# Class-C values move to the first two slots of a causal mixer, gates take their place, and a minimum is pinned

## The chip, the cores and the metric

The kernel runs on one core of a Trainium2 chip. The metric is the device time of one execution in microseconds. A core has five engines with queues of their own, each in order: TensorE for matrix products (PE; PEld are its weight loads), VectorE (DVE), ScalarE (ACT), GpSimd (POOL) and SyncE (SP), whose queue issues most DMAs. Products go to PSUM, which has eight banks of 128 x 512 floats.

## The reference

One decoder layer on 512 tokens of width 1024, in fp32. After an RMSNorm, one projection W_in feeds three mixers and three gates per channel:

- A: twelve heads of causal, dilated attention in three groups (dilation 1, 4, 16). Head slot j of all three groups is combined by the softmax denominators.
- B: a gated linear recurrence of width 512.
- C: eight heads of causal attention over blocks of 256.

```
gt = sigmoid(gates)
merged = gt[0]*(o_a @ p_a) + gt[1]*(o_b @ p_b) + gt[2]*(o_c @ p_c)
x = x + merged @ w_out
x = x + (silu(gate) * up) @ w_down        # gate, up from rms_norm(x) @ w_gu
```

A last RMSNorm follows. A and C add a relative-position bias from one table.

## The kernel before, in words

Every fp32 product is made of three: both operands are split into a rounded high part and the low rest (hi, lo), and `mm3` adds hi·hi, hi·lo and lo·hi. A weight chunk of 128 x 1024 is loaded by SP (`wraw`), rounded on ScalarE (`whi`, L177) and its rest taken on GpSimd, or on VectorE for the first and last chunks (`wlo`, L178). `chunk_plan` lists the chunks in the order of their use; three buffers hold raw chunks and four the split ones, so the loader runs two chunks ahead.

The projections of mixer A start before the norm is known: they run on `X`, the raw input times the norm's weights, and the norm's factor is applied when a result leaves PSUM. `norm_tok` makes the factor per token (`r_tok`), `norm_all` spreads it by two matmuls over all partitions (`rb`, L359, L361). Later `renorm` multiplies a second copy of the input, which `reload` fetches, by `rb` (L924) and splits it (L244, L245) into `XN`; all later projections run on `XN`. `bias_rows` multiplies the bias table with one-hot rows (L391), adds a mask (L393) and writes the rows to DRAM; `bias_tile` reads shifted tiles back through SP's queue (L401).

Mixer A goes by four head slots, d0 to d3. For one slot j:

- `ea` (through `fa`) evicts a projection of queries or keys into tiles (L469 to L524).
- `la` makes the logits of the three groups: group 0 by L554, L555 and the reduction L562, groups 1 and 2 by L576, L579 and the reductions L585. `stn` and `stp` take the minima (the logits are negated).
- `wa` takes exponentials (L594) and sends minima and sums to DRAM (`exch`, issued on ScalarE at L717), from where SP's queue reads them back in the other group's token order (L719).
- `wa2` takes the minimum over both (`mm`, L725), its factors (df, ee, wd, ds, rd, ff; L727 to L740), and scales the tiles P by them (L599).
- `ta` transposes P on TensorE (L608, L622) and `xa` multiplies with the values (L659, L777).

`weave(gen, n, steps, first)` runs a projection of n steps and puts the given steps between its matmuls, evenly, after the first `first`. `class_values_g` makes the values of groups 1 and 2, `values_g` four token blocks of one value projection in 32 steps of three matmuls, on `X` for group 0 and on `XN` for mixer C (`VC`, used later by `tc_`). A gate is a projection of 24 matmuls with a tanh behind it; `early(place)` makes as many gates as the table EARLY lists, and what is left of the 24 is made in the merge.

The engines' orders are not those of the program text: a scheduler moves instructions within each engine's queue where no dependence forbids it, by its own estimate of times. `tc.keep_in_program_order` holds one instruction at its place in the text. PSUM banks are taken as they come free: a product that needs one waits for the engine that empties it. TensorE's queue is in order, so everything behind such a product waits too.

Of the kernel before, what the change touches and what calls it, by code (L numbers as in the profile page):

```python
# [43 lines left out]
N_POOL = 62  # L44
AHEAD = 2

EARLY = {"a2": 1, "a3": 1, "v0": 1, "v1": 1, "c0": 1, "c1": 1, "l1": 1, "l2": 1, "l3": 1, "l4": 1,
         "b0": 1, "b1": 4}
G_LEAD = 2
N_WARM = 10  # L50
# [5 lines left out]
def chunk_plan():  # L56

    plan = []

    def a(h, i, w):  # L60
        plan.append(("ma", (OFF_QA, OFF_KA)[w], A_PAIRS[h][i]))

    def v(off, g):
        plan.extend(("v", off + g * 256, kh) for kh in range(2))

    def c(m, w):
        plan.append(("m", "w_in", (OFF_QC, OFF_KC)[w] + m * 128))

    def b(m):
        plan.append(("m", "w_in", OFF_XB + m * 128))  # L70
        plan.append(("m", "w_in", OFF_GB + m * 128))

    gates = [("m", "w_in", OFF_GT + n * D + m * 128) for m in range(8) for n in range(3)]

    def g(place):
        for _ in range(EARLY[place]):
            plan.append(gates.pop(0))

    for n in (0, 1):
        a(0, n, 0)  # L80
        a(0, n, 1)
    v(OFF_VA, 0)
    plan.extend(("vv", OFF_VA + 256, kq) for kq in range(4))
    a(0, 2, 0)
    a(0, 2, 1)
    for n in range(2):
        a(1, n, 0)
        a(1, n, 1)
    a(1, 2, 0)
    g("a2")  # L90
    a(1, 2, 1)
    g("a3")
    v(OFF_VC, 0)
    g("v0")
    v(OFF_VC, 1)
    c(0, 0)
    g("v1")
    c(0, 1)
    g("c0")
    c(1, 0)  # L100
    c(1, 1)
    g("c1")
    for m in (2, 3):
        c(m, 0)
        g("l1" if m == 2 else "l3")
        c(m, 1)
        g("l2" if m == 2 else "l4")
    b(0)
    g("b0")
    plan.append(("lru",))  # L110
    for m in range(1, 4):
        b(m)
    g("b1")
    np_ = 0
    for m in range(8):
        while gates and 24 - len(gates) < 3 * m + 3 + G_LEAD:
            plan.append(gates.pop(0))
        while np_ * 8 < (m + 1) * 10:
            plan.append(("p", np_))
            np_ += 1  # L120
    for m in range(8):
        plan.append(("m", "w_out", m * 128))
    for m in range(FT):
        plan.append(("m", "w_gu", m * 128))
        plan.append(("m", "w_gu", FFN + m * 128))
    for k in range(FT):
        plan.append(("d", k))
    return plan


def layer_kernel(tc, x0p, xT, wts, tab, oneh, msk, idn, gfin, out):
# [4 lines left out]
    with (  # L136
# [20 lines left out]
        def f32(ap):  # L157
            return ap.bitcast(F32)
# [40 lines left out]
        def weave(gen, n, steps=(), first=0):  # L199

            done = 0
            i = 0
            while True:
                try:
                    next(gen)
                except StopIteration as e:
                    for st in steps[done:]:
                        st()
                    return e.value
                i += 1  # L210
                while done < len(steps) and i - first >= (done + 1) * (n - first) / (len(steps) + 1):
                    steps[done]()
                    done += 1
# [205 lines left out]
                        yield  # L419
            return [[ps[:, g * 256 : g * 256 + 256] for ps in pss] for g in range(2)]  # L420

        def values_g(act=X):
            ch = [chunk("v"), chunk("v")]
            outs = []
            for tb in range(4):
                if tb % 2 == 0:
                    ps = bank()
                o = ps[:, (tb % 2) * 256 : (tb % 2) * 256 + 256]
                outs.append(o)
                t = slice(tb * 128, (tb + 1) * 128)  # L430
                for k in range(8):
                    hi, lo = ch[k // 4]
                    c = slice((k % 4) * 256, (k % 4) * 256 + 256)
                    xh, xl = act[k]
                    mm3(o, xh[:, t], xl[:, t], hi[:, c], lo[:, c], k == 0, k == 7)
                    yield
            return outs

        def values_mm(steps=(), first=0, act=X):
            return weave(values_g(act), 32, steps, first)  # L440

        def values_out(outs, perm=False, scaled=False):
            res = []
            for tb, o in enumerate(outs):
                o4 = o.rearrange("p (h e) -> p h e", h=4)
                v = slot(F32R, "v")
                v4 = v.rearrange("p (h two e) -> p h two e", two=2, e=E)
                if scaled:
                    nc.scalar.copy(v4[:, :, 0, :], o4)
                    nc.vector.tensor_sub(v4[:, :, 1, :], o4, f32(v4[:, :, 0, :]))  # L450
                    res.append(v)
                    continue
                rt = r_tok[:, tb + 4 * perm : tb + 4 * perm + 1]
                nc.scalar.activation(v4[:, :, 0, :], o4, AF.Copy, scale=rt)
                nc.vector.scalar_tensor_tensor(
                    v4[:, :, 1, :], in0=o4, scalar=rt, in1=f32(v4[:, :, 0, :]),
                    op0=ALU.mult, op1=ALU.subtract,
                )
                res.append(v)
            return res  # L460
# [200 lines left out]


        VA = []
        qk = {}
        exch = dr.tile([4, 4 * 512], F32)

        def ea(ps, half, i, w, scaled=False):
            pair = A_PAIRS[half][i]
            perm = [g > 0 for g, _ in pair]
            r = None if scaled else (rq, rb)[w]  # L670
            t = (q_tiles, k_tiles)[w](ps, r, perm)
            for n in range(2):
                qk[pair[n] + (w,)] = t[n]

        def fa(half, i, w, steps=(), first=0):
            scaled = (half, i) > (1, 0)
            ea(project(XN if scaled else X, "ma", steps, first), half, i, w, scaled)

        def st_part(st, s, o):
# [41 lines left out]
        def wa2(d):  # L721

            for st, gs in ((d["stn"], (0,)), (d["stp"], (1, 2))):
                mm = sm.tile([128, 4], F32, name=uid("mm"), tag="mm")
                nc.vector.tensor_tensor(mm, st[:, 0:4], st[:, 8:12], op=ALU.min)  # L725
                df = sm.tile([128, 8], F32, name=uid("df"), tag="df")
                nc.vector.tensor_sub(df[:, 0:4], mm, st[:, 0:4])  # L727
                nc.vector.tensor_sub(df[:, 4:8], mm, st[:, 8:12])
                ee = sm.tile([128, 8], F32, name=uid("ee"), tag="ee")
                nc.scalar.activation(ee, df, AF.Exp)  # L730
                wd = sm.tile([128, 8], F32, name=uid("wd"), tag="wd")
                sums = st.rearrange("p (o s c) -> p o s c", o=2, s=2)[:, :, 1, :]
                nc.vector.tensor_mul(wd.rearrange("p (o c) -> p o c", o=2),
                                     ee.rearrange("p (o c) -> p o c", o=2), sums)
                ds = sm.tile([128, 4], F32, name=uid("ds"), tag="ds")
                nc.vector.tensor_add(ds, wd[:, 0:4], wd[:, 4:8])
                rd = sm.tile([128, 4], F32, name=uid("rd"), tag="rd")
                nc.vector.reciprocal(rd, ds)
                ff = sm.tile([128, 4], F32, name=uid("ff"), tag="ff")
                nc.vector.tensor_mul(ff, rd, ee[:, 0:4])  # L740
                for g in gs:
                    scale_p(d["lay"][g], ff)
# [44 lines left out]
                OA.append(split(oa[j // 2]))  # L787


        VC = []  # L790
        qkc = {}
        OC = []

# [110 lines left out]
        def gate(steps=()):  # L904
            ng[0] += 1
            z = slot(F32, "z")
            nc.scalar.activation(z, project(XN, "m", steps), AF.Tanh, scale=0.5)
            return z
# [19 lines left out]
        zs = []  # L928
        ng = [0]

        def early(place):
            for _ in range(EARLY[place]):
                zs.append(gate())


        f0 = project2(X, "ma", 1)
# [11 lines left out]
        nc.vector.tensor_scalar(out=rq, in0=rb, scalar1=Q_SCALE, scalar2=None, op0=ALU.mult)  # L948
        for n, (i, w) in enumerate(((0, 0), (0, 1), (1, 0), (1, 1))):
            ea(f0[n], 0, i, w)  # L950
        bias_rows()
        VA.append(values_out(weave(va0, 32)))
        reload()
        d0, st = la(0)
        for outs in weave(class_values_g(), 32, st):
            VA.append(values_out(outs, True))
        wa(d0)
        fa(0, 2, 0)
# [1 line left out]
        wa2(d0)  # L960
        renorm(range(8))
        d1, st = la(1)
        fa(1, 0, 0, st, 3)
        wa(d1)
        st = ta(d0)
        fa(1, 0, 1, st)
        fa(1, 1, 0)
        xa(d0)
        wa2(d1)
        fa(1, 1, 1)  # L970
        st = ta(d1)
        fa(1, 2, 0, st)
# [4 lines left out]
        wa(d2)  # L977
        early("a3")
        d3, st = la(3)
        VC.append(values_out(values_mm(st, 16, act=XN), scaled=True))  # L980
        wa2(d2)
        wa(d3)
        st = ta(d2)
        early("v0")
        VC.append(values_out(values_mm(st, act=XN), scaled=True))
        fc(0, 0)
        early("v1")
        xa(d2)
        wa2(d3)
        fc(0, 1)  # L990
# [344 lines left out]
```

## Time and profile before

| | us |
|---|---|
| median of three runs | 924.76 (923.46 to 925.12) |
| the profiled execution | 924.81 |
| its span, first to last instruction | 923.0 |
| TensorE busy | 886.4 |
| VectorE busy | 480.8 |
| ScalarE busy | 400.6 |
| GpSimd busy | 245.9 |
| mean granted TensorE clock | 0.980 |

A page or an answer of the trace names an instruction by its line, engine and operation, then the tile written and the tiles read. In a row of the waits view stand the waiting engine and line, what released it, the time in all, the number of waits and the longest. In a row of the timeline stand start, duration, instruction, count, and in brackets the idle time ahead and what ended it. Matmuls overlap in the trace, so what one costs is read from the distance between two starts.

### The profile page before, as it was taken

The page shows a single profiled execution, that of the slowest core. Times are in us where ns is not written, and L with a number is a line of the kernel's source. Part 1 is how long each engine was busy: PE and PEld are TensorE (multiplying, and loading weights), DVE is VectorE, ACT ScalarE, POOL GpSimd, SP SyncE. Part 2 cuts the span into 40 slices and gives each one's busy share as a digit, 9 for nine tenths or more (in the row PEclk, how much of TensorE's full clock was granted, in tenths as well). Part 3 has the DMA queues.
Part 4 walks back from the last instruction along what each step waited for, and adds up shares of the span by engine and source line. Part 5 has one row for each costly group of instructions (what it writes and reads, how often), then busy time and mean ns, then how long its engine had stood idle before and what let it go on. Part 6 is the DMA issues. An engine that isn't in the chain of part 4 may idle for free.

```text
span 923.0 us, 11073 instructions
## 1 busy us (share of the span) xinstructions
PE 886.4 (96%) x4166; PEld 744.6 (81%) x4166; DVE 480.8 (52%) x924; ACT 400.6 (43%) x692; POOL 245.9 (27%) x163
## 2 busy tenths in 40 slices
PE   9989479999999999999999999999999999999996
PEld 7888358888888888878888888888888888888885
DVE  7495976545564666765334554544444444422226
ACT  7374565545666647862322443433333322211113
POOL 1142324335443332457111131122211111100004
PEclk9999689999999999999999999999999999999999
DMA  7245131363322222222323322222232222222302
GB/s 279 76 148 109 64 95 64 87 80 116 112 83 80 92 92 69 76 99 100 115 92 108 120 92 92 92 92 91 96 110 92 92 97 108 92 92 92 110 27 92
DMA packets 40278, 90.27 MB, mean 98 GB/s; under 512 B 13988, under 2 KB 15780, under 8 KB 40224
## 3 DMA queue, kind: packets, MB, share of 16 engines
q1 hardware_dynamic: 34048, 88.26, 28.9%
q10 hardware_dynamic: 5824, 0.98, 0.6%
q8 instruction: 33, 0.54, 0.3%
q0 software_dynamic: 352, 0.33, 0.1%
q14 instruction: 21, 0.17, 0.1%
HBM read 87.34 MB, written 2.20 MB: 97 GB/s over the span
## 4 chain that ended last, share of the span: by engine, by line
PE 76%; DVE 9%; ACT 5%; DMA 5%; issue 4%; POOL 0%; DVEq 0%; ACTq 0%; POOLq 0%; SPq 0%
PE ps L196 20%; PE ps L195 20%; PE ps L197 20%; PE ps L1182 11%; DMA exch<-stp 2%; ACT P L594 1%; PE ps L608 1%; PE ps L659 1%; DMA stn<-exch 1%; DVE xt L924 1%; DVE gb L898 1%; DVE lo L245 1%; PE ps L555 1%; DMA xt<-in_xT 1%; PE ps L554 1%
## 5 line engine op out<-in xcount | busy, mean ns | idle before, releaser
L177 ACT CAST whi<-wraw 128x1024 fp32r<-128x1024 f32 (+1 forms) x149 | 154.6, 1039 | 271.5 <-issue 106.8
L195 PE MATMUL ps<-hi,whi 128*128 128x512 f32 x504 | 200.2, 398 | 1.1 <-ACT hi L247 1.1
L178 POOL TENSOR_TENSOR wlo<-wraw,whi 128x1024 fp32r<-128x1024 f32 x55 | 135.0, 2459 | 242.9 <-ACT whi L177 231.5
L196 PE MATMUL ps<-lo,whi 128*128 128x512 f32 x504 | 197.6, 392 | 0.2 <-DVE lo L248 0.2
L197 PE MATMUL ps<-hi,wlo 128*128 128x512 f32 x504 | 197.3, 391 | 0.0
L178 DVE TENSOR_TENSOR wlo<-wraw,whi 128x1024 fp32r<-128x1024 f32 (+1 forms) x94 | 116.9, 1245 | 123.7 <-ACT whi L177 123.7
L195 PE MATMUL ps<-uhi,whi 128*128 128x512 f32 x352 | 137.9, 392 | 0.0
L197 PE MATMUL ps<-uhi,wlo 128*128 128x512 f32 x352 | 137.1, 389 | 0.0
L196 PE MATMUL ps<-ulo,whi 128*128 128x512 f32 x352 | 136.9, 389 | 0.0
L195 PEld LDWEIGHTS ps<-hi,whi 128*128 128x128 f32 x504 | 95.4, 189 | 20.0 <-ACT hi L247 1.6
L197 PEld LDWEIGHTS ps<-hi,wlo 128*128 128x128 f32 x504 | 95.3, 189 | 20.2
L196 PEld LDWEIGHTS ps<-lo,whi 128*128 128x128 f32 x504 | 95.5, 189 | 18.9 <-DVE lo L248 0.5
L1156 POOL TENSOR_TENSOR av<-sg,uu 128x512 f32<-128x512 f32 x22 | 45.7, 2079 | 198.5 <-DVE sg L1154 198.5
L197 PEld LDWEIGHTS ps<-uhi,wlo 128*128 128x128 f32 x352 | 66.1, 188 | 14.0
L196 PEld LDWEIGHTS ps<-ulo,whi 128*128 128x128 f32 x352 | 66.1, 188 | 13.4
L195 PEld LDWEIGHTS ps<-uhi,whi 128*128 128x128 f32 x352 | 66.1, 188 | 13.4
L1182 PE MATMUL ps<-wlo,hi 128*128 128x512 f32 (+1 forms) x180 | 57.7, 384 | 0.0
L1182 PE MATMUL ps<-whi,lo 128*128 128x512 f32 (+1 forms) x180 | 57.7, 384 | 0.0
L1182 PE MATMUL ps<-whi,hi 128*128 128x512 f32 (+1 forms) x180 | 57.1, 384 | 0.0
L1152 DVE TENSOR_TENSOR uu<-ps,rb 128x512 f32<-128x512 f32 x22 | 15.2, 691 | 64.9 <-PE ps L197 64.9
L1182 PEld LDWEIGHTS ps<-whi,lo 128*128 128x128 f32 x180 | 33.8, 188 | 6.8
L1182 PEld LDWEIGHTS ps<-wlo,hi 128*128 128x128 f32 x180 | 33.8, 188 | 6.7
(240 smaller groups left out, 1267.0 us busy)
## 6 DMA issues: line engine op xcount, KB each, us to landing
wraw<-in_wts SPq DMA_DIRECT2D x145, 512.0 KB, 3.2
xt<-in_xT SPq DMA_DIRECT2D x15, 256.0 KB, 5.3
bias<-relb SPq DMA_DIRECT2D x8, 256.0 KB, 6.9
xr<-in_xT SPq DMA_DIRECT2D x8, 256.0 KB, 2.6
out<-y SPq DMA_DIRECT2D x7, 256.0 KB, 2.2
wraw<-in_wts SPq DMA_DIRECT2D x4, 256.0 KB, 4.8
bias<-relb SPq DMA_DIRECT2D x4, 128.0 KB, 4.7
bias<-relb SPq DMA_DIRECT2D x8, 64.0 KB, 5.2
```

Of the source, the lines that this page charges most:

```text
L177: nc.scalar.copy(hi[:, cc], raw[:, cc])
L178: eng.tensor_sub(lo[:, cc], raw[:, cc], f32(hi[:, cc]))
L195: nc.tensor.matmul(o, lh, rh, start=start, stop=False)
L196: nc.tensor.matmul(o, lh, rl, start=False, stop=False)
L197: nc.tensor.matmul(o, ll, rh, start=False, stop=stop)
L245: nc.vector.tensor_sub(lo, src, f32(hi))
L554: nc.tensor.matmul(bk, qh[:, qc], kk[:, k0 : k0 + nn], start=True, stop=False)
L555: nc.tensor.matmul(bk, ql[:, qc], kk[:, k0 : k0 + nn], start=False, stop=True)
L594: nc.scalar.activation(lay[qb][0], lay[qb][0], AF.Exp, scale=-1.0, bias=negm[:, qb : qb + 1], accum_out=den[:, qb : qb + 1])
L1152: nc.vector.tensor_mul(uu, pu, r2)
L1156: nc.gpsimd.tensor_mul(av, sg, uu)
L1182: nc.tensor.matmul((acc[tb][hf] if o is None else o)[:, cc], l[:, t], r[:, hf * 512 + cc.start : hf * 512 + cc.stop], start=((k == 0 or fi ...
```

## The change

Three things change in the program, beside the tables that follow from them.

1. The two projections of mixer C's values move from slots d2 and d3 to slots d0 and d1. There they run on X, with the norm's factor at the eviction like group 0's values; the form without a factor (`scaled`) goes. The projection `fa(1, 0, 0)` moves behind them and runs on XN. In the places that the values leave, d2 and d3 get gates: v0 and v1 have two each and a new place v2 has one. 18 gates are made ahead of the merge, before it were 15; the logits of d3 are woven into the second gate of v0, the transposes of d2 into the second of v1.
2. The minimum `mm` of `wa2` is pinned to its place in the program's order.
3. `bias_rows` comes ten value steps later, and d0's logits begin after twelve of the 32 steps of the class values rather than at once.

```diff
-EARLY = {"a2": 1, "a3": 1, "v0": 1, "v1": 1, "c0": 1, "c1": 1, "l1": 1, "l2": 1, "l3": 1, "l4": 1,
+EARLY = {"a2": 1, "a3": 1, "v0": 2, "v1": 2, "v2": 1, "c0": 1, "c1": 1, "l1": 1, "l2": 1, "l3": 1, "l4": 1,
          "b0": 1, "b1": 4}
...
         def fa(half, i, w, steps=(), first=0):
-            scaled = (half, i) > (1, 0)
+            scaled = half == 1
...
-                nc.vector.tensor_tensor(mm, st[:, 0:4], st[:, 8:12], op=ALU.min)
+
+                tc.keep_in_program_order(
+                    nc.vector.tensor_tensor(mm, st[:, 0:4], st[:, 8:12], op=ALU.min))
...
-        def early(place):
-            for _ in range(EARLY[place]):
-                zs.append(gate())
+        def early(place, steps=()):
+
+            n = EARLY[place]
+            for i in range(n):
+                zs.append(gate(steps if i == n - 1 else ()))
...
+        for _ in range(10):
+            next(va0)
         bias_rows()
         VA.append(values_out(weave(va0, 32)))
         reload()
         d0, st = la(0)
-        for outs in weave(class_values_g(), 32, st):
+        for outs in weave(class_values_g(), 32, st, 12):
             VA.append(values_out(outs, True))
         wa(d0)
         fa(0, 2, 0)
...
         d1, st = la(1)
-        fa(1, 0, 0, st, 3)
+        VC.append(values_out(values_mm(st, 12)))
         wa(d1)
         st = ta(d0)
-        fa(1, 0, 1, st)
+        VC.append(values_out(values_mm(st)))
+        fa(1, 0, 0)
+        xa(d0)
+        fa(1, 0, 1)
+        wa2(d1)
         fa(1, 1, 0)
-        xa(d0)
-        wa2(d1)
         fa(1, 1, 1)
...
         d3, st = la(3)
-        VC.append(values_out(values_mm(st, 16, act=XN), scaled=True))
+        early("v0", st)
         wa2(d2)
         wa(d3)
         st = ta(d2)
-        early("v0")
-        VC.append(values_out(values_mm(st, act=XN), scaled=True))
+        early("v1", st)
         fc(0, 0)
-        early("v1")
+        early("v2")
         xa(d2)
```

How the change stands in the engines' orders is shown at three places. The first is VectorE's queue where it evicts fa(0,2,0) and fa(0,2,1) (qt, ql, kt, kk) and meets d0's minima (mm, from the tiles stn and stp; df, wd, ff are its factors). Before:

```order
L725 TENSOR_TENSOR mm_888<-stn_583 128x4
L725 TENSOR_TENSOR mm_907<-stp_584 128x4
L455 SCALAR_TENSOR_TENSOR v_773<-ps_587,mixr_358,v_773 128x4x64
L727 TENSOR_TENSOR df_890<-mm_888,stn_583 128x4
```

and further down in the same queue, with the scaling of P between:

```order
L479 TENSOR_TENSOR qt_831<-ps_806,rq_409 128x512
L738 RECIPROCAL rd_899<-ds_897 128x4
L738 RECIPROCAL rd_918<-ds_916 128x4
L740 TENSOR_TENSOR ff_901<-rd_899,ee_893 128x4
L740 TENSOR_TENSOR ff_920<-rd_918,ee_912 128x4
L599 TENSOR_SCALAR P_622<-P_622,ff_901 128x128
```

And now (the line numbers are those of the changed kernel):

```order
L475 TENSOR_TENSOR qt_831<-ps_806,rq_409 128x512
L451 SCALAR_TENSOR_TENSOR v_779<-ps_589,mixr_358,v_779 128x4x64
L465 TENSOR_TENSOR ql_834<-qt_831,qh_833 64x512 x2
L465 TENSOR_TENSOR qq_839<-qt_831,qq_839 64x512
L475 TENSOR_TENSOR kt_873<-ps_848,rb_407 128x512
L520 TENSOR_TENSOR kk_875<-kt_873,kk_875 64x512
L515 TENSOR_TENSOR kk_878<-kt_873,kk_878 64x2x128 x2
L515 TENSOR_TENSOR kk_883<-kt_873,kk_883 64x2x128 x2
L724 TENSOR_TENSOR mm_888<-stn_583 128x4
L246 TENSOR_TENSOR lo_932<-xt_117_567,hi_931 128x512
L726 TENSOR_TENSOR df_890<-mm_888,stn_583 128x4
```

The evictions now stand ahead of the first minimum; the second, of stp, stands behind seven of the eight low halves of XN. The second place is TensorE's queue behind fa(0,2,1), whose result is ps_848; the weights that follow are those of fa(1,0,0) before:

```order
L195 MATMUL ps_848<-xhi_152,whi_729 128x512
L196 MATMUL ps_848<-xlo_154,whi_729 128x512
L197 MATMUL ps_848<-xhi_152,wlo_730 128x512
L195 MATMUL ps_979<-xhi_104,whi_801 128x512
L196 MATMUL ps_979<-xlo_106,whi_801 128x512
```

and of mixer C's values now:

```order
L196 MATMUL ps_848<-xhi_152,whi_714 128x512
L197 MATMUL ps_848<-xlo_154,whi_714 128x512
L198 MATMUL ps_848<-xhi_152,wlo_715 128x512
L196 MATMUL ps_985<-whi_801,xhi_104 128x256
L197 MATMUL ps_985<-wlo_802,xhi_104 128x256
```

Before, 24 matmuls stand between fa(0,2,1) and d1's logits; now 51 of half the width do, and the other 45 of the same projection stand between and behind the logits. The third place is VectorE's queue in d0's logits, where TensorE waits for banks (xt is the reloaded input, P and m the reductions of the class logits):

```order
L922 SCALAR_TENSOR_TENSOR xt_122_577<-xt_122_577,prm,rb_407 128x512
L922 SCALAR_TENSOR_TENSOR xt_123_579<-xt_123_579,prm,rb_407 128x512
L922 SCALAR_TENSOR_TENSOR xt_124_581<-xt_124_581,prm,rb_407 128x512
L581 ISA P_694,m_127_585<-ps_695,P_694 128x128
L581 ISA m_127_585 128x1
```

All eight tiles xt stand ahead of the first of these reductions now; before, the last two stood behind the first pair.

More of the change, by code (lines that the diff above doesn't have):

```diff
@@ L85, in chunk_plan @@
     a(0, 2, 1)
+    v(OFF_VC, 0)
+    v(OFF_VC, 1)
     for n in range(2):
@@ L92, in chunk_plan @@
     g("a3")
-    v(OFF_VC, 0)
     g("v0")
-    v(OFF_VC, 1)
+    g("v1")
     c(0, 0)
-    g("v1")
+    g("v2")
     c(0, 1)
@@ L420, in class_values_g, with values_g @@
             return [[ps[:, g * 256 : g * 256 + 256] for ps in pss] for g in range(2)]
-        def values_g(act=X):
+        def values_g():
             ch = [chunk("v"), chunk("v")]
@@ L433, in values_g @@
                     c = slice((k % 4) * 256, (k % 4) * 256 + 256)
-                    xh, xl = act[k]
+                    xh, xl = X[k]
                     mm3(o, xh[:, t], xl[:, t], hi[:, c], lo[:, c], k == 0, k == 7)
@@ L437, in values_g, with values_mm, values_out @@
             return outs
-        def values_mm(steps=(), first=0, act=X):
-            return weave(values_g(act), 32, steps, first)
-        def values_out(outs, perm=False, scaled=False):
+        def values_mm(steps=(), first=0):
+            return weave(values_g(), 32, steps, first)
+        def values_out(outs, perm=False):
             res = []
@@ L447, in values_out @@
                 v4 = v.rearrange("p (h two e) -> p h two e", two=2, e=E)
[L448 to L452, printed above, removed]
                 rt = r_tok[:, tb + 4 * perm : tb + 4 * perm + 1]
@@ L663, in layer_kernel @@
         VA = []
+        VC = []
         qk = {}
@@ L787, in xa @@
                 OA.append(split(oa[j // 2]))
-        VC = []
         qkc = {}
```

## The prediction

> **What bounds the kernel now.** I read the page's busy shares first, then a table by stage, then the waits, and last VectorE's and TensorE's rows around the holes that the table shows. On the page TensorE is busy nearly throughout:
>
> ```profile
> PE 886.4 (96%) x4166; PEld 744.6 (81%) x4166; DVE 480.8 (52%) x924; ACT 400.6 (43%) x692; POOL 245.9 (27%) x163
> ```
>
> The change adds and removes no matmul, so it can only win or lose in TensorE's idle time and in the stretches where its clock is granted at half. The table by stage, cut at the holes, finds both (columns: stretch, length, busy PE, PEld, DVE, ACT, POOL with counts, granted clock, DMA share, GB/s):
>
> ```profile
> 40.00:60.70 20.70, 19.44 (x107) 18.28 (x107) 18.57 (x24) 16.12 (x22) 6.25 (x5) 1.00 0.14 37
> 60.70:63.80 3.10, 0.01 (x1) 0.01 (x1) 2.50 (x6) 1.11 (x3) 0.00 (x0) 1.00 0.65 158
> 63.80:67.60 3.80, 3.77 (x10) 3.08 (x11) 3.00 (x4) 3.26 (x4) 3.06 (x2) 0.56 1.05 401
> ...
> 94.50:106.70 12.20, 0.09 (x1) 0.02 (x1) 11.29 (x22) 5.18 (x8) 5.34 (x2) 0.66 0.24 87
> 106.70:115.30 8.60, 8.03 (x26) 6.77 (x27) 7.96 (x10) 7.00 (x12) 2.82 (x1) 0.50 0.00 0
> 115.30:129.50 14.20, 13.06 (x64) 10.05 (x62) 11.97 (x39) 11.09 (x34) 3.69 (x4) 1.00 0.33 80
> 129.50:134.60 5.10, 0.14 (x2) 0.08 (x1) 1.03 (x8) 0.63 (x4) 1.36 (x1) 0.79 0.67 202
> 134.60:139.30 4.70, 4.70 (x12) 3.73 (x13) 4.62 (x20) 4.10 (x8) 0.00 (x0) 0.50 0.02 6
> ...
> 180.30:186.80 6.50, 2.76 (x20) 2.31 (x19) 6.45 (x24) 1.57 (x4) 3.17 (x4) 1.00 0.18 71
> 186.80:190.70 3.90, 3.90 (x17) 3.70 (x18) 3.90 (x20) 1.99 (x9) 0.00 (x0) 0.56 0.00 2
> 190.70:409.80 219.10, 217.96 (x1112) 184.81 (x1110) 129.47 (x286) 138.82 (x263) 90.09 (x61) 1.00 0.30 91
> ```
>
> Idle in these rows up to 190.70, length minus PE busy: 1.26 + 3.09 + 0.03 + 12.11 + 0.57 + 1.14 + 4.96 + 3.74 = 26.9 us. The lost clock, PE busy times (1 - clock) in the four slow rows: 3.77 x 0.44 = 1.7, 8.03 x 0.50 = 4.0, 4.70 x 0.50 = 2.4, 3.90 x 0.44 = 1.7, together 9.8. So **36.7 us** can be won here; after 190.70 only 1.1 us in 219 is idle.
>
> The waits over the stretch up to 330 say what the holes wait for:
>
> ```profile
> DVE mm L725 <- DMA stn<-exch: 29.8, 4, 12.2
> ...
> PE ps L554 <- DVE kk L524: 12.1, 1, 12.1
> ...
> PE ps L777 <- DVE df L728: 5.0, 1, 5.0
> ...
> PE ps L576 <- DVE v L455: 3.1, 1, 3.1
> ```
>
> The largest hole is VectorE's queue. These are its rows, then two steps of the chain of waits:
>
> ```profile
> 92.34 0.16 DVE L725 TENSOR_TENSOR mm<-stn 128x4 f32<-128x4 f32 x1 [6.06 <-DMA stn<-exch]
> ...
> 94.31 0.68 DVE L479 TENSOR_TENSOR qt<-ps,rq 128x512 f32<-128x512 f32 x1
> ...
> 104.50 0.69 DVE L479 TENSOR_TENSOR kt<-ps,rb 128x512 f32<-128x512 f32 x1
> 105.88 0.69 DVE L524 TENSOR_TENSOR kk<-kt,kk 64x512 fp32r<-64x512 f32 x1 [0.68 <-ACT kk L523]
> ```
> ```profile
> 83.24 6.44 DMA exch<-stp
> 89.74 2.58 DMA stn<-exch
> ```
>
> The minimum of slot 0 stands in VectorE's queue ahead of qt and kt, the evictions of the projections that slot 1's logits need. It holds them for 6.06 us until the exchange is back, then the scaling of twelve P tiles goes first, and TensorE, with all its work behind those logits, stands for 12.1 us. Slot 1's minimum makes the 5.0 us hole in the same way, and slot 2's the 3.7 us at 180.30.
>
> **The change part by part.** *The pin.* All four pairs of minima now stand where the program has them: slot 0's behind the whole eviction of fa(0,2,1), slot 1's behind that of fa(1,0,1), slots 2 and 3's behind the work ahead of theirs. It costs no instruction.
>
> *Slot 0's values* (two projections of class-C values, 96 matmuls each) now run on X right behind fa(0,2,1), where fa(1,0,0) stood, and fa(1,0,0) runs on XN. Their matmul durations are the starts' distance in these rows:
>
> ```profile
> 48.10 0.51 PE L195 MATMUL ps<-whi,xhi 128*128 128x512 f32 x1
> ...
> 55.96 0.39 PE L197 MATMUL ps<-whi,xlo 128*128 128x512 f32 x1
> ...
> 78.09 0.39 PE L195 MATMUL ps<-xhi,whi 128*128 128x512 f32 x1
> ...
> 191.21 0.39 PE L197 MATMUL ps<-hi,wlo 128*128 128x512 f32 x1
> ...
> 195.28 0.39 PE L197 MATMUL ps<-hi,wlo 128*128 128x512 f32 x1
> 195.51 0.28 PE L195 MATMUL ps<-whi,hi 128*128 128x256 f32 x1
> ...
> 197.90 0.28 PE L197 MATMUL ps<-whi,lo 128*128 128x256 f32 x1
> ```
>
> 195.28 less 191.21 over 18 steps is 0.226 us; 197.90 less 195.51 over 20 is 0.120; for the class values 55.96 less 48.10 over 33 is 0.238. So a value projection is 11.5 us, a 24-matmul projection or gate 5.4 us. Their sum is what it was: what moves is cover. Scaling at the eviction costs VectorE nothing new beside the subtraction that it replaces.
>
> *Slots 2 and 3.* Three gates (16.3 us) and two that stood there already take the values' 23 us. Slot 2's minimum now follows slot 3's logits: behind slot 2's own stand the rest of a projection (4.1), products (1.9), three gates (16.3) and slot 3's logits (1.9), 24 us. Slot 3's has two gates, a projection, another gate (21.7 us) and slot 2's products. An exchange that takes 9.0 us behind some 6 us of reductions and exponentials, as slot 0's, fits into both; so I take them as covered, as slot 1's is by 11.5 + 5.4 + 5.4 us. If a cover fails, the old holes return: 5.0 + 2.4 for slot 1, 3.7 + 1.7 for slot 2.
>
> *The bias rows and ten value steps.* Sixteen value matmuls stand between the two norm matmuls (+1.9 us) and the three bias matmuls follow, so rb comes about 0.6 us later than now (1.9 less the two bias matmuls of 1.3 that stand there now), and TensorE fills the 1.26 us that it idles. The class values then start near 48.1 - 1.3 = 46.8. SP's queue now takes one more weight chunk ahead of the three bias tiles and two bias tiles ahead of the eight xt loads; GpSimd splits that chunk before it writes the rows. I cost this at nothing: in the stretch 60.70 to 67.60 the DMA is filled now by two chunks that no longer start there.
>
> *What is late next* is VectorE, which from rb to the end of slot 0's logits works without a break. Its rows there:
>
> ```profile
> 63.19 0.88 DVE L455 SCALAR_TENSOR_TENSOR v<-ps,mixr,v 128x256 fp32r<-128x256 f32 x2 [0.54 <-ACT v L454]
> 64.87 0.48 DVE L455 SCALAR_TENSOR_TENSOR v<-ps,mixr,v 128x256 fp32r<-128x256 f32 x1 [0.80 <-ACT v L454]
> 65.27 5.66 DVE L924 SCALAR_TENSOR_TENSOR xt<-xt,prm,rb 128x512 f32<-128x512 f32 x3
> ...
> 75.17 3.25 DVE L924 SCALAR_TENSOR_TENSOR xt<-xt,prm,rb 128x512 f32<-128x512 f32 x2
> 78.34 0.28 DVE L585 CUSTOM_DVE_ANT_0 P<-ps,P 128x128 f32<-128x128 f32 x1
> ```
>
> *Hole A.* TensorE reaches slot 0's first class logits at 46.8 + 66 x 0.238 + 8 logits x 0.120 = 63.5. It needs two banks there, which the v rows free at 63.6 and 65.35, now 0.6 later: 66.0. Idle about 2.4 us beside the two logits between, and I add 1.7 of lost clock as the row 63.80 has it: **4.1 us** (now 3.1 + 1.7).
>
> *Hole B, new.* fa(0,2,0) takes the bank that the first class reduction frees, and in the new order all eight xt scalings stand ahead of it (now six). The old rows finish eight xt at 78.34; the same work 0.6 later and two reductions gives 79.4. TensorE is there 30 matmuls and four pairs of logits later, at 66.0 + 7.1 + 0.5 + 1.7, near 75.4. Idle 4.0 plus 1.7: **5.7 us**. From below: if the clock is kept and VectorE is 2 us quicker, 2; from above: 3.5 us more for VectorE and 4.0 of lost clock, 12.
>
> *The rest of slot 1.* fa(0,2,0) and fa(0,2,1) take 10.9 us + 1.7, so the values start at 79.4 + 12.6 = 92.0 (now 78.09 + 10.9 = 89.0 for the same place), and slot 1's logits are due at 92.0 + 51 x 0.120 = 98.1, against 106.7. VectorE has evicted kt and kk by about 95, so they do not wait. Behind them VectorE makes XN's low halves:
>
> ```profile
> 109.84 7.09 DVE L245 TENSOR_TENSOR lo<-xt,hi 128x512 fp32r<-128x512 f32 x8
> ```
>
> From about 97 these 7.1 us and some 1.5 us of minima and scaling end at 105.6; TensorE wants the first of slot 1's banks at 98.1 + 1.9 + 45 x 0.120 = 105.4. I keep 0.5 us for it.
>
> **Sum:** 36.7 - 4.1 - 5.7 - 0.5 = 26.4 us less. The profiled execution took 924.81 us (span 923.0 and 1.8 around it), 0.05 above the median of the three runs, 924.76. That gives 898.4; for small waits that I cannot see I add 0.6: **899 us**.
>
> The slow clock after the 12.1 us hole lasted 8.6 us in the row above, after 3.1 us of idling 3.8. The Trainium skill, "TensorE: Matmul & The Clock Gate", section "What's actually happening", gives about 3.4 us of sustained work for the return to full clock, so 1.7 us lost at each hole. By that alone the four losses would be 6.8 and the time 902; the row decides for me, since the logits there came with gaps between them.
>
> **Rivals.** *VectorE's backlog takes half of it.* GpSimd's splits slow VectorE: the same two products of 128x4 took
>
> ```profile
> 94.91 2.35 POOL L178 TENSOR_TENSOR wlo<-wraw,whi 128x1024 fp32r<-128x1024 f32 x1 [7.05 <-ACT whi L177]
> ...
> 95.12 2.23 DVE L740 TENSOR_TENSOR ff<-rd,ee 128x4 f32<-128x4 f32 x2
> ...
> 136.16 0.24 DVE L740 TENSOR_TENSOR ff<-rd,ee 128x4 f32<-128x4 f32 x2
> ```
>
> that is 2.0 us more for the first pair, while GpSimd's split ran. I counted as many collisions as now. With two more in the chain to hole B and two more between 97 and 105.6, B grows by 4 and slot 1's bank comes 4 late with 2 of lost clock: 899 + 10 = 909. The Trainium skill, "SBUF — State Buffer", section "Who interferes with whom", says that a GpSimd instruction reading SBUF and a VectorE one with two SBUF inputs exclude each other for a whole instruction; the moved splits come earlier, onto other VectorE work, which is this rival.
>
> *Given back in the merge.* Three gates fewer are left for the merge, 16.3 us of cover. If VectorE or GpSimd then held the merge: 899 + 16 = 915. Against it: from 190.70 on VectorE is busy 129.5 of 219.1 us, GpSimd 90.1.
>
> *Holes A and B do not open* (VectorE fast enough): 924.8 - 36.7 + 1 = 889.
>
> *Slower.* The table of bias rows goes through DRAM to SP's queue, with xt loads and weight chunks behind it, and GpSimd's writes now stand behind one more split. If rows come late, slot 0's logits, the bank of hole B and the first exchange come late with them, us for us. The tiles have slack, as this step of the chain of waits shows:
>
> ```profile
> 58.00 3.66 DMA bias<-relb
> ```
>
> VectorE reads them behind the three xt of 65.27, at 70.9, some 9 us after they landed. To end above 924.8 the rows must lose 9 + 26 = 35 us, say 40, for 930. One split costs 2.4; nothing in the trace has that size.
>
> *The pin does nothing:* then the exchange would have to come back after about 97, with slot 1's reductions behind it. ScalarE issues the write at 83.24 now; 1.1 us later by hole B and some 2 for value casts that now stand ahead of it, plus 6.4 and 2.6, gives 95.4; 5 us more would give 904, within the forecast's range.
>
> **How the numbers follow.** Forecast 0.62 (own range 894 to 904, from the bounds of B and the small waits), backlog 0.18, merge 0.08, no holes 0.07, slower 0.03, no change left 0.02. The range 890 to 912 takes in the forecast, all but the end of the backlog, and reaches nearly to the case without holes. A change of 0.2% (1.8 us) is about what a measurement of this kernel can tell. Faster is the sum of the first four, 0.95, same 0.02, slower 0.03.
>
> **What would show it.** Right: no TensorE wait on kk or df above 1 us; slot 1's logits near 98; mm waiting under 1 us in all for stn; two holes near 64 and 76, each with half clock behind it, fa(0,2,0) at about 79. Wrong: a hole above 3 us after 100, a wait of mm on the exchange, idle TensorE in the merge (about 280 to 384), or VectorE reaching the first class reduction later than 82.

## The result, and the profile after

| | before | changed |
|---|---|---|
| median of four runs, us | 924.94 (923.46 to 926.89) | 902.31 (902.25 to 905.68) |
| profiled execution's span, us | 923.0 | 900.5 |
| TensorE busy, us | 886.4 | 881.0 |
| mean granted TensorE clock | 0.980 | 0.991 |

The ratio is 0.9763, with a 95% interval from 0.9734 to 0.9792: 22.6 us faster. The forecast was 899, its range 890 to 912. Of the span's 22.5 us, TensorE's idle time gives 17.1 (36.6 less 19.5), and its busy time, which holds the same 4166 matmuls at a better clock, 5.4.

The waits of TensorE up to 404 us, where the merge begins to use the mixers' outputs (waiting line, what released it, us in all, times, the longest):

```profile
PE ps L618 <- DVE P L595: 3.9, 3, 2.6
PE ps L196 <- DVE m L581: 2.9, 1, 2.9
PE ps L572 <- DVE v L451: 2.1, 2, 1.2
PE ps L196 <- ACT hi L248: 1.1, 1, 1.1
PE ps L572 <- DVE stn L558: 0.4, 1, 0.4
PE ps L196 <- DVE stn L558: 0.3, 1, 0.3
```

The 12.1 us on kk and the 5.0 on df are gone. Row three is the old hole A, row two is hole B, which the prediction had foreseen. Row four is the merge's first product (1.1 us in the kernel before too). Row one was not foreseen: slot 2's class transposes (`flip_pairs`, L618) wait for the scaling of P. I call it hole C. (Lines have moved by up to four: mm is L724, ee L729, the scaling of P L595, the logits' reductions L558 and L581.) The table by stage, cut at these holes, with the prediction's columns:

```profile
0.00:40.00 40.00, 38.75 (x201) 33.64 (x202) 24.01 (x72) 21.11 (x31) 6.87 (x13) 1.00 0.58 204
40.00:62.60 22.60, 22.59 (x110) 20.60 (x108) 20.91 (x27) 15.98 (x23) 6.45 (x5) 1.00 0.28 74
62.60:69.00 6.40, 4.30 (x13) 3.60 (x14) 5.34 (x5) 4.12 (x6) 4.79 (x2) 0.73 1.04 390
69.00:75.50 6.50, 6.10 (x26) 5.47 (x25) 6.50 (x17) 3.77 (x11) 1.39 (x2) 1.00 0.58 140
75.50:78.46 2.96, 0.01 (x2) 0.03 (x1) 2.96 (x8) 0.00 (x0) 1.84 (x1) 1.00 0.11 4
78.46:82.50 4.04, 4.04 (x11) 3.17 (x12) 3.31 (x18) 2.80 (x13) 0.00 (x0) 0.58 0.38 4
...
104.60:113.50 8.90, 8.22 (x69) 8.06 (x68) 8.86 (x38) 8.50 (x32) 5.06 (x4) 1.00 0.36 68
113.50:194.80 81.30, 81.30 (x418) 68.94 (x418) 50.47 (x154) 47.47 (x118) 36.80 (x23) 1.00 0.39 102
194.80:201.30 6.50, 3.00 (x12) 2.06 (x12) 6.05 (x17) 2.38 (x5) 3.56 (x4) 0.76 0.63 114
201.30:206.00 4.70, 4.70 (x15) 3.65 (x14) 2.04 (x6) 1.52 (x4) 0.00 (x0) 0.61 0.65 221
206.00:404.00 198.00, 196.89 (x965) 164.97 (x963) 125.14 (x255) 126.39 (x227) 77.90 (x54) 1.00 0.24 84
404.00:900.50 496.50, 489.02 (x2187) 405.22 (x2186) 214.38 (x279) 149.09 (x197) 97.31 (x55) 1.00 0.27 95
```

Idle time plus lost clock, as the prediction counted them: A 2.1 + 1.2; B 2.95, 0.4 just ahead of it and 1.7 behind; slot 1's stretch from 104.60 0.7 (0.3 for its bank, 0.4 for slot 0's transposes); C 3.5 (6.50 less 3.00) + 0.7 + 1.8. From 206 on only 1.1 us is idle up to the merge. From there to the end 7.5 us are idle, and 7.4 in the kernel before (from 409.80).

How C comes about stands in the rows of three engines. VectorE and ScalarE, around slot 2's two minima:

```profile
180.65 2.36 DVE L246 TENSOR_TENSOR lo<-oa,hi 128x512 fp32r<-128x512 f32 x1 [5.69 <-ACT hi L245]
182.93 0.28 DVE L558 CUSTOM_DVE_ANT_0 P<-ps,bias 128x128 f32<-128x128 f32 x1
...
187.68 0.16 DVE L724 TENSOR_TENSOR mm<-stn 128x4 f32<-128x4 f32 x1
...
191.53 0.15 DVE L732 TENSOR_TENSOR wd<-ee,stn 128x8 f32<-128x8 f32 x1
...
193.32 2.34 DVE L724 TENSOR_TENSOR mm<-stp 128x4 f32<-128x4 f32 x1
...
197.01 3.75 DVE L595 TENSOR_SCALAR P<-P,ff 128x128 f32<-128x128 f32 x8
```
```profile
186.52 0.40 ACT L590 ACTIVATE P<-P,stp 128x128 f32<-128x128 f32 x1 [1.30 <-DVE stp L581]
...
191.05 0.19 ACT L729 ACTIVATE ee<-df 128x8 f32<-128x8 f32 x1
```

GpSimd, and TensorE's two rows:

```profile
193.23 2.41 POOL L179 TENSOR_TENSOR wlo<-wraw,whi 128x1024 fp32r<-128x1024 f32 x1 [1.65 <-ACT whi L178]
...
198.05 2.43 POOL L179 TENSOR_TENSOR wlo<-wraw,whi 128x1024 fp32r<-128x1024 f32 x1 [2.12 <-ACT whi L178]
```
```profile
197.44 1.23 PE L618 MATMUL ps<-ident,P 128*128 128x128 f32 x5 [2.62 <-DVE P L595]
...
200.62 0.69 PE L618 MATMUL ps<-ident,P 128*128 128x128 f32 x2 [0.88 <-DVE P L595]
```

Four things add up. VectorE stands idle for 5.69 us before the low part of oa, the outputs of slots 0 and 1, which only the merge needs; slot 3's reductions (from 182.93) queue behind it. The pinned first minimum comes behind them, at 187.68, and finds the exchange long back. ScalarE has ee behind eight exponentials of slot 3, so the factors start some 3 us later, at 191.05. And the second minimum takes 2.34 us instead of 0.16, exactly while GpSimd splits a weight chunk, as do the eight scalings (3.75; 1.66 at slot 0). TensorE wants the scaled tiles at 194.8 and gets them from 197.

The kernel before already shows oa in the way. There the rounding of oa, ahead of its low part, waits in ScalarE's queue for GpSimd's sums, and behind it stands the eviction of a gate, for whose bank TensorE waited 2.58 us, the larger part of slot 2's old hole:

```profile
185.46 0.62 ACT L244 CAST hi<-oa 128x512 fp32r<-128x512 f32 x1 [3.06 <-POOL oa L785]
186.10 0.60 ACT L907 ACTIVATE z<-ps 128x512 f32<-128x512 f32 x1
```

### The profile page after: what moved, and what is told of

Same layout as the page of the kernel before. It is cut to its first block, busy times and chain, and to the rows that moved or that the text cites. A ratio compares the mean times of both kernels' runs of the same rounds, so it can differ in the third digit from the quotient of the medians.

```text
span 900.5 us, 11072 instructions
## 1 busy us (share of the span) xinstructions
PE 881.0 (98%) x4166; PEld 739.8 (82%) x4166; DVE 489.2 (54%) x922; ACT 398.8 (44%) x692; POOL 249.6 (28%) x163
## 4 chain that ended last, share of the span: by engine, by line
PE 82%; DVE 10%; ACT 5%; issue 1%; DMA 1%; SPq 0%; DVEq 0%; ACTq 0%
PE ps L196 22%; PE ps L197 22%; PE ps L198 21%; PE ps L1185 12%; PE ps L655 1%; PE ps L604 1%; DVE xt L922 1%; DVE gb L896 1%; PE ps L551 1%; ACT whi L178 1%; PE ps L550 1%; ACT P L590 1%; DVE P L595 1%; DMA xt<-in_xT 1%; DVE a L891 1%
## 5 line engine op out<-in xcount | busy, mean ns | idle before, releaser
L196 PE MATMUL ps<-hi,whi 128*128 128x512 f32 x520 | 206.3, 397 | 1.1 <-ACT hi L248 1.1
L197 PE MATMUL ps<-lo,whi 128*128 128x512 f32 x520 | 203.8, 392 | 0.2 <-DVE lo L249 0.2
L198 PE MATMUL ps<-hi,wlo 128*128 128x512 f32 x520 | 203.6, 392 | 0.0
L198 PEld LDWEIGHTS ps<-hi,wlo 128*128 128x128 f32 x520 | 98.2, 189 | 20.7
L196 PEld LDWEIGHTS ps<-hi,whi 128*128 128x128 f32 x520 | 98.4, 189 | 20.4 <-ACT hi L248 1.5
L197 PEld LDWEIGHTS ps<-lo,whi 128*128 128x128 f32 x520 | 98.4, 189 | 19.4 <-DVE lo L249 0.5
L196 PE MATMUL ps<-whi,xhi 128*128 128x256 f32 (+1 forms) x128 | 40.7, 322 | 0.3 <-DVE stn L558 0.3
L197 PE MATMUL ps<-wlo,xhi 128*128 128x256 f32 (+1 forms) x128 | 40.9, 319 | 0.0
```

The costliest lines, as they stand in the source:

```text
L196: nc.tensor.matmul(o, lh, rh, start=start, stop=False)
L197: nc.tensor.matmul(o, lh, rl, start=False, stop=False)
L198: nc.tensor.matmul(o, ll, rh, start=False, stop=stop)
```

## The experiments

All kernels compute the whole reference. Each ratio is against the kernel before in the same comparison (medians 923.65 to 924.04 there, 924.94 in the first one), so a difference of medians between two comparisons can be off by some 1.3 us. Up to about 63 us the profiles differ by up to 1.9 us without a difference in the code: the first class logits stand at 63.4 to 65.3 in kernels whose code is the same up to there. So I compare lengths of holes, not absolute times between profiles.

### The pin alone, and everything but the pin

The first kernel is the one before with only `tc.keep_in_program_order(...)` around mm; the second is the changed one without it:

```diff
-                tc.keep_in_program_order(
-                    nc.vector.tensor_tensor(mm, st[:, 0:4], st[:, 8:12], op=ALU.min))
+                nc.vector.tensor_tensor(mm, st[:, 0:4], st[:, 8:12], op=ALU.min)
```

> The kernel before with the pin of the minimum and nothing else. Theory (the pin takes the exchange out of VectorE's queue, but the matmuls that cover it are needed too): slot 0's minimum no longer stands ahead of qt and kt, but slot 1's logits still follow fa(0,2,1) directly, so TensorE waits there for the eviction of kt and kk, about 6 us instead of 12.1; slot 1's hole (5.0 and 2.4 of clock) goes; slot 2's (3.7 and 1.7) stays: about 909 us (905 to 914). Rival one, the pin carries the whole gain and the values' move is only rearrangement: 902 to 904. Rival two, the pin only shifts the stall from VectorE to TensorE's products: 918 to 925.

Measured: 922.44 us, ratio 0.9984 (0.9975 to 0.9993). My theory and the first rival fell; the second rival held. The three largest waits of TensorE up to 330 in this kernel:

```profile
PE ps L622 <- DVE P L599: 10.5, 2, 8.1
PE ps L608 <- DVE P L599: 7.8, 2, 5.6
PE ps L608 <- issue: 3.3, 1, 3.3
```

The wait on kk fell from 12.1 to 1.0, so the pin did take the exchange out of VectorE's way. But transposes of slots 0 and 1 now wait for scaled tiles, 18.3 us. Slot 0's second factor comes at 117.02, behind slot 1's reductions, and TensorE has only one projection to fill the time.

> The changed kernel without the pin; values, gates and bias rows as changed. Theory: slot 0's minima stand ahead of kt again and bring the scaling of twelve P tiles with them, so kt and kk come some 4 us later and slot 1's logits wait; the exchange itself is covered, since its reads land near 92 and VectorE reaches qt at 86 to 92; with lost clock about 905 to 909. Slot 2's minima then stand before slot 3's reductions, which may take the hole of 3.5 us near 197 away. Rival: the values' cover is the whole gain and the pin is without effect, 901 to 903; a second rival: the pin is what costs the hole near 197, and without it the kernel is faster, 896 to 899.

Measured: 912.86 us, 0.9887 (0.9873 to 0.9900), the theory's direction, 4 us beyond its range. The two largest waits of TensorE:

```profile
PE ps L775 <- DVE pp L625: 7.7, 3, 5.3
PE ps L550 <- DVE kk L520: 4.6, 1, 4.6
```

and VectorE at slot 0 and slot 1:

```profile
90.46 0.16 DVE L723 TENSOR_TENSOR mm<-stn 128x4 f32<-128x4 f32 x1 [3.32 <-DMA stn<-exch]
...
98.39 0.69 DVE L475 TENSOR_TENSOR kt<-ps,rb 128x512 f32<-128x512 f32 x1
...
127.96 0.16 DVE L723 TENSOR_TENSOR mm<-stn 128x4 f32<-128x4 f32 x1 [7.75 <-DMA stn<-exch]
```

Not the wait of 3.3 us alone costs here: the scaling of nine P tiles goes ahead of kt. What I had left out was slot 1, where the minimum holds the evictions of slot 0's transposes for 7.75 us, and five scalings, which take 5.51 us beside splits of GpSimd, hold the last of them longer. The same comes once more at slot 3, where the minimum waits 12.02 us and TensorE 1.8 near 222. So the parts work together: the pin alone gives 1.5 us, the rest without it 11, both together 22.6.

### Hole C

> The changed kernel with three gates at v1 and none at v2, so slot 2's transposes of the class tiles come one gate (5.4 us) later on TensorE and nothing else moves. Theory (the hole of 2.62 and 0.88 us near 197 to 200, with half clock behind it, is slot 2's factors coming late behind ScalarE's exponentials of slot 3 and a slowed minimum): the hole and its lost clock, 3.5 + 2.5 us, go: 896.3 us (895.5 to 897.5). Rival: the products of slot 2 then wait for the evictions of the transposes, or slot 3's exchange is no longer covered, and the 6 us come back there: 901 to 904.

The edit is one line:

```diff
-EARLY = {... "v0": 2, "v1": 2, "v2": 1, ...
+EARLY = {... "v0": 2, "v1": 3, "v2": 0, ...
```

Measured: 901.62 us, 0.9769 (0.9756 to 0.9783), no difference from the changed kernel that these runs can tell: the rival. Two waits of 1.6 and 1.5 us remain, slot 2's and now slot 3's, both for L595. The transposes came only some 3 us later, not 5.4, and the scalings took 3.94 us beside a split of GpSimd. The gate that slot 2 gained is one that slot 3 lost: moving cover did not pay. What delays the tiles was still open.

> The changed kernel with slot 3's logits woven into the first of the two gates of v0 instead of the second. Everything that ScalarE and VectorE do for slot 3's logits comes 5.4 us earlier, and slot 2's minima and factors behind it. Theory (the hole near 197 is this queue): it goes, 896.3 us (895.5 to 897.5). Rival one: slot 2's exchange is not back when the minimum stands at the head of VectorE's queue (about 182 instead of 187.7; its second read was issued at 177.0), so the minimum waits and TensorE with it: 900 to 903. Rival two: slot 3's logits find no free banks 5.4 us earlier: 899 to 902.

```diff
-                zs.append(gate(steps if i == n - 1 else ()))
+                zs.append(gate(steps if i == (n - 1 if last else 0) else ()))
...
-        early("v0", st)
+        early("v0", st, False)
```

Measured: 902.99 us, 0.9783 (0.9769 to 0.9796): the second rival's mechanism, no free banks, 1 us above its range. The first rival's range holds the time, but the minimum did not wait for the exchange. Hole C went, and this stands in its place:

```profile
183.26 0.77 PE L196 MATMUL ps<-hi,whi 128*128 128x512 f32 x1 [4.36 <-DVE stn L558]
```

The logits came 5.4 us earlier, but the reductions that empty their banks did not: they still stood behind the low part of oa, at 181.87. That pointed to oa as the cause.

> The changed kernel with the split of the first pair of head outputs (oa, slots 0 and 1) moved in the program from slot 1's products to behind the second gate of v1; the merge is the first to need it. Theory: VectorE stands idle 5.69 us before that subtraction (it waits for ScalarE's rounding, which waits for GpSimd's sums), and slot 3's reductions, the second minimum and slot 2's factors queue behind it; with it out of the way all of these come about 3 us earlier, the hole of 2.62 + 0.88 us near 197 and its half clock go: 897 us (895.5 to 898.5). Rival: the hole is made by GpSimd's split slowing the second minimum (2.34 us instead of 0.16) and by ScalarE's exponentials; then 2 us of it stay, with the clock loss: 900 to 902.

```diff
-            if j % 2 == 1:
+            if j % 2 == 1 and now:
                 OA.append(split(oa[j // 2]))
...
-        xa(d1)
+        xa(d1, False)
...
         early("v1", st)
+        OA.append(split(oa[0]))
```

Measured: 896.53 us, 0.9701 (0.9686 to 0.9715), 5.8 us less than the changed kernel; the theory said 897. VectorE:

```profile
178.82 0.29 DVE L558 CUSTOM_DVE_ANT_0 P<-ps,bias 128x128 f32<-128x128 f32 x1 [2.59 <-PE ps L551]
...
184.54 0.15 DVE L724 TENSOR_TENSOR mm<-stn 128x4 f32<-128x4 f32 x1
...
193.88 1.66 DVE L595 TENSOR_SCALAR P<-P,ff 128x128 f32<-128x128 f32 x8
```

The reductions wait for TensorE's logits alone, the minimum comes 3.1 us earlier, though this profile's start is 1.3 us later, and TensorE's waits on L618 fall from 3.9 us to 0.4, with no wait above 0.3 us from 115 to the merge. The minimum is 4.4 us earlier at an equal start, more than the 3.5 us that TensorE stood idle in C. The subtraction in the wrong place of VectorE's queue is shown as the root of C; the meeting with GpSimd, which lengthened the minimum, is a part of it (here it hits wd, 1.88 us, and does no harm).

> The changed kernel with the pin on the minima of slots 0, 1 and 3, not on slot 2's. Theory (at slot 2 the pin itself makes the hole near 197, since it holds the minima behind slot 3's reductions): slot 2's minima stand ahead of these again and wait there for the exchange some 4 us, with GpSimd's sums and slot 3's reductions behind them, but TensorE has two gates there and does not run dry; the hole of 3.5 us and its clock loss go: 896.3 us (895.5 to 898). Rival: slot 3's reductions come some 5 us later by it, its exchange too, and slot 3's transposes or products wait in place of slot 2's, 2 to 4 us with lost clock: 899 to 902.

```diff
-        wa2(d2)
+        wa2(d2, False)
```

The new argument leaves out the pin. Measured: 901.12 us, 0.9756 (0.9740 to 0.9773): the rival. At slot 2 the minimum waits for the exchange, ahead of slot 3's reductions:

```profile
180.26 0.17 DVE L723 TENSOR_TENSOR mm<-stn 128x4 f32<-128x4 f32 x1 [4.68 <-DMA stn<-exch]
```

C is gone, but slot 3's class transposes wait 1.8 us, with the clock at 0.70 in the 5.6 us behind, and its class logits 1.4 us for a bank. At this slot pin or no pin is the same delay, handed to another slot.

### VectorE between 40 and 113 us

> The changed kernel with the last three of the eight scalings of the second input copy (xt) held, in VectorE's order, behind slot 0's reductions and exponential sums instead of ahead of the class reductions. Theory (hole B, 2.95 us near 76 with half clock behind it, is these three scalings standing ahead of the reduction that frees the bank): hole B and its clock loss go, 2.95 + 0.4 + 1.7 us: 897.5 us (896.5 to 899). Rival (VectorE has a backlog as a whole from 40 to 113, so what is taken from one place comes back at slot 1's logits or banks, near 97 to 105): 900 to 903.

```diff
+        rescale(range(5, 8), True)
         fa(0, 2, 0)
         fa(0, 2, 1)
         wa2(d0)
+        rescale(range(5), False)
         renorm(range(8))
```

The scalings of xt 5 to 7 are pinned behind `wa(d0)`, those of xt 0 to 4 stay free, and `renorm` keeps only the splits. Measured: 901.91 us, 0.9758 (0.9743 to 0.9773): the rival, no gain. Hole B is gone, fa(0,2,0) starts without a wait, and slot 1's bank takes the time:

```profile
104.34 0.35 PE L196 MATMUL ps<-whi,xhi 128*128 128x256 f32 x1 [2.08 <-DVE stn L558]
```

with a clock of 0.64 behind it, 1.7 us in 4.7. VectorE is busy for 67 of the 73.5 us from 40 to 113.5 in the changed kernel; here the order that serves one bank earlier served the next one later.

> The changed kernel with three of the weight splits (the two that GpSimd ran at 64.2 to 69.4 and the one at 74.5 to 77.3) on VectorE, where such a split takes 1.22 us. It measures what GpSimd's splits cost VectorE there: the eight scalings of xt and what stands between took 12.9 us, against 7.8 us by their durations elsewhere. Theory (they exclude each other): the scalings shrink to 0.7 us each and the three splits add 3.7, so VectorE reaches the first class reduction 1.4 us earlier than 77.8 and hole B falls from 2.95 to about 1.5: 900 us (898 to 902). Rival (the scalings are slow by themselves): VectorE comes 3.7 us later, 906 to 909. Second rival (the splits wait in VectorE's order for ScalarE's rounding or the load and hold what is behind them): 904 to 912.

```diff
-            eng = nc.gpsimd if 6 < i < N_POOL else nc.vector
+            eng = nc.gpsimd if 6 < i < N_POOL and i not in (10, 11, 12) else nc.vector
```

Measured: 899.87 us, 0.9744 (0.9728 to 0.9760), in the theory's range. These runs alone can't tell that from the changed kernel's 0.9763 (0.9734 to 0.9792); the profile, and the runs with the later oa below, can. VectorE reached the first class reduction 3.9 us earlier (73.94), not 1.4, hole B went whole, and 2.0 us came back at slot 1's bank. The first three scalings of xt, in the changed kernel and in this one:

```profile
64.94 5.64 DVE L922 SCALAR_TENSOR_TENSOR xt<-xt,prm,rb 128x512 f32<-128x512 f32 x3
```
```profile
66.73 2.07 DVE L922 SCALAR_TENSOR_TENSOR xt<-xt,prm,rb 128x512 f32<-128x512 f32 x3
...
74.36 1.22 DVE L179 TENSOR_TENSOR wlo<-wraw,whi 128x1024 fp32r<-128x1024 f32 x1
```

So a split on GpSimd (2.4 us there) cost VectorE about 1.8 us in each such meeting, more than the 1.22 us of doing it itself; the last three took 4.16 with one split beside them. The Trainium skill, "SBUF — State Buffer", section "Who interferes with whom", says that a VectorE instruction with two SBUF inputs and a GpSimd one that reads SBUF exclude each other; the pair 5.64 against 2.07, and the minimum of 2.34 us, agree.

### The bias rows

> The changed kernel with the third part undone: the bias rows stand ahead of the value steps again, and slot 0's logits begin at the first class-value step. Theory (the part only fills the 1.3 us that TensorE idled at 40 to 42): 903.5 us (902.5 to 905). Rival one (the later logits are what keeps hole A at 2.1 us instead of 3.1 and the bank free): 904.5 to 907. Rival two (the later bias rows cost as much as they win): 901 to 902.5.

```diff
-        for _ in range(10):
-            next(va0)
         bias_rows()
...
-        for outs in weave(class_values_g(), 32, st, 12):
+        for outs in weave(class_values_g(), 32, st):
```

Measured: 903.50 us, 0.9772 (0.9754 to 0.9791), 1.2 us above the changed kernel, as the theory said, but within what the runs can tell. Its waits are other ones: 1.3 us at 41 to 42 come back, one at slot 0's class logits grows from 0.4 to 1.2, hole B is gone and slot 1's bank waits 2.1. From 40 to 113 us the waits alone sum to 6.6 us against 5.7: the third part mostly moves waits.

### Together

> The later split of oa together with the three weight splits on VectorE. Theory (the two holes are separate): the gains add, 896.5 - 2.4 = 894.1 us (893 to 895.5). Rival (VectorE, earlier by some 4 us at slot 1, only meets the next limit): 895.5 to 897.

> As late3, with the three splits that follow (GpSimd ran them at 85.3 to 90.6 and 92.2 to 94.6) on VectorE too. They slowed ql, qq and kk: 3.61 us for two ql against 1.38, 1.47 for kk against 0.69, 2.55 for the four kk behind. Theory (the splits exclude VectorE's two-input instructions): VectorE pays 3.7 us and wins about 4.5 at this place, so the hole of 2.0 us near 101, where slot 1's first reduction frees a bank late, shrinks by about 1 us: 893 us (891.5 to 894.5). Rival (three splits in VectorE's order wait for ScalarE's rounding or hold kt): 895 to 899.

> As late6, with the two splits before (GpSimd ran them at 45.0 to 47.6 and 49.3 to 51.7, beside kk) on VectorE too. By durations they cost 2.4 us there and give back 1.4 + 2.0 us (kk took 2.04 instead of 0.69 us, the next four 4.54 instead of 2.5). Theory: another 0.5 to 1 us earlier for VectorE at holes A and slot 1's bank: 892.5 us (891 to 894). Rival (hole A waits for the eviction of the values, which these splits do not hold): no change against late6. Second rival: the first keys come later by 1.2 us and the bias rows with them: 1 to 2 us slower than late6.

The edits are those of the later oa and of the splits, with the tuples (10, 11, 12), (10, ..., 15) and (8, ..., 15). Measured:

| kernel | us | ratio to before |
|---|---|---|
| oa later, three splits | 892.65 | 0.9667 (0.9650 to 0.9684) |
| oa later, six splits | 892.68 | 0.9666 (0.9649 to 0.9683) |
| oa later, eight splits | 895.91 | 0.9702 (0.9684 to 0.9719) |

The first beats the changed kernel by 9.7 us (8.9 by the ratios); it came 1.5 below the expected 894.1, about what two comparisons can be off by. Against the later oa alone (0.9686 to 0.9715) its interval lies apart, so the three splits do help. Between 60 us and the merge it still has these waits of TensorE, and none above 0.3 us beside them:

```profile
PE ps L572 <- DVE v L451: 1.8, 2, 0.9
PE ps L196 <- DVE stn L558: 1.8, 1, 1.8
PE ps L196 <- DVE m L581: 1.4, 1, 1.4
```

With six splits slot 1's bank no longer waits, but four scalings meet GpSimd (4.32 us instead of 1.07) and slot 0's transposes wait 2.2 us instead: no gain over three. The time lies in the theory's range only because three splits had reached it already. With eight, hole A is gone, but B grows to 5.1 us:

```profile
77.14 0.77 PE L196 MATMUL ps<-xhi,whi 128*128 128x512 f32 x1 [5.06 <-DVE m L581]
```

The second rival held there, with 3.2 us lost to six splits, not 1 to 2. SyncE issues the first bias tile 1.0 us later than with six and the first xt load behind them 2.8 us later, and VectorE waits 1.88 us for xt, which no other of these kernels does.

## Why the prediction was right, and where not

- **The 36.7 us to win** and what frees them: right. The waits on kk and df are gone, no minimum waits for the exchange, and the merge gives nothing back (7.5 us idle from 404 to the end against 7.4). In this kernel the merge runs from about 404 to 486, though, not from 280 to 384 as the sign for it said.
- **Holes A and B:** right in place and cause, a little small. A cost 3.3 (forecast 4.1), B 5.05 (5.7). TensorE reached B at 75.5 (75.4), VectorE's reduction came at 77.8 (79.4). Slot 1's logits stood at 97.1 (98.1), its bank cost 0.3 (0.5), and slot 0's transposes 0.4 that was not in the sum.
- **rb 0.6 us later:** right, but hidden in these two profiles. VectorE's first use of rb starts at 40.27, before at 41.03, since the granted clock of the first 40 us was 1.00 against 0.96, worth 1.6 us that I had not counted. In the four later profiles with the clock at 0.96 there and the same code up to there it starts at 41.5 three times (`logits_first`, `oa_late`, `pin_013`) and at 42.1 once (`xt_behind`), 0.5 and 1.1 later. Of the eleven profiled kernels with the later bias rows, four had 0.96 there and seven 1.00, so I take the 1.6 us as the start's spread, which is luck; but all three without them had 0.96, so a part of the change in it is not excluded.
- **"I take them as covered"** (slots 2 and 3): this step failed, by 6.05 us at slot 2. The exchange was covered, as the step said: the minimum did not wait. The step compared TensorE's 24 us of work with the exchange and the work ahead of it, and took everything between the minimum and the transposes as free. In VectorE's in-order queue the pinned minimum follows slot 3's reductions, these follow the low part of oa, and in ScalarE's queue ee follows eight exponentials. Moving oa alone wins 5.8 us back. The price that the prediction named for a failed cover at slot 2, 3.7 + 1.7, was near.
- **The sum:** 36.7 - 3.3 - 5.05 - 0.7 - 6.05 + 1.6 = 23.2 against 22.5 in the profiles; 0.7 us in small waits is not assigned. That 899 came near 902 owes something to A, B and the start being milder than counted.
- **The rivals:** the backlog is real, but the meetings of GpSimd and VectorE stand in the kernel before as well (xt 5.66 us for three there), so it did not add 10 us. The price of 2.0 us for one meeting was right (1.8 measured). "The pin does nothing" needed the exchange back after about 97; it was back at 90.5 in the kernel without the pin, 5 us ahead of the 95.4 worked out there. And the pin does much: without it the kernel takes 10.6 us longer, mostly through what is scaled or held behind the minimum.
- **The signs:** those named for a right forecast came (kk and df, slot 1's logits, mm, the two holes, fa(0,2,0) at 78.5). One of those named for a wrong forecast came too, nearly: a hole of 2.62 and 0.88 us after 100, in two pieces.

## What to carry to other kernels

Cover for a round trip must be counted in every in-order queue between its return and the consumer, not only on the bounding engine: write down what stands in each queue ahead of each step. An instruction that nobody needs soon, but that waits for a slow engine, can cost more than the wait that was tuned away; look for idle time of VectorE ahead of a late-needed tile. Pinning and moving cover belong together: alone they gave 1.5 and 11 us here, together some 22.

## What the runs showed of the hardware that was not expected

- Whether a short hole costs clock differed from profile to profile. Behind every hole of 2.6 us or more between 60 us and the merge the granted clock of the next 5 us was 0.50 to 0.74. Of shorter ones, 2.20 us (six splits) and 2.11 (bias rows back) kept the clock at 1.00 in the 5 us behind, while 2.08 (xt behind) and 1.79 (no pin) lost it, and two of 0.9 us lost it in one kernel (0.61, three splits) and not in another (1.00, with oa later). The Trainium skill, "TensorE: Matmul & The Clock Gate", section "What's actually happening", says that the activity window runs freely and does not reset when a kernel starts; that agrees with this spread, though no run here shows the window itself.
- A scaling of P has one SBUF tile and one factor per partition as inputs, and it meets GpSimd's splits too: 3.75, 3.94 (three gates at v1) and 3.76 us for eight, each with a split of 2.4 us beside it, against 1.66 where GpSimd ran none. I had counted only two-input instructions.
